# Modulation's products traced a step behind their transfers, and its bias loaded a job ahead

## The chip, the cores and the metric

The kernel runs on one core of a Trainium2 chip. The core has a matrix engine (TensorE, PE in the rows; PEld is its loading of stationary operands), three engines for elementwise work (VectorE or DVE, ScalarE or ACT, GpSimd or POOL) and SyncE (SP), which here only issues DMA transfers. Each engine works through its own queue in order and waits at the head of it for semaphores. The metric is the device time of one execution in microseconds, the median of several runs.

## The reference

The input is a sequence of 256 tokens with 1024 features. Nine sublayers change it in turn: two pre-norm layers (feed-forward, mixer, feed-forward) and one modulated layer (feed-forward, token mixer, feed-forward).

```python
for layer in range(2):
    x = x + 0.5 * swiglu(rmsnorm(x, norm_g[layer, 0]), w_in, w_out)
    x = x + mixer(rmsnorm(x, norm_g[layer, 1]))      # HGRN2, then forgetting attention
    x = x + 0.5 * swiglu(rmsnorm(x, norm_g[layer, 2]), w_in, w_out)

mod = (silu(c) @ w_ada + b_ada).reshape(b, 3, 3, 1024)
def sublayer(h, i, fn, resid_w):
    shift, scale, gate = mod[:, i, 0], mod[:, i, 1], mod[:, i, 2]
    u = rms_norm(h, norm_pre[i]) * (1.0 + scale) + shift
    return h + resid_w * gate * rms_norm(fn(u), norm_post[i])
```

The change touches only `mod`: a vector of 1024 features (c after silu) times a matrix of 1024 x 9216, plus a bias row. All is float32.

## The kernel before

The residual stream stays in SBUF as two tiles of 128 tokens. A projection has the transposed activations as the stationary operand and streams the weights, in k-tiles of 128 rows. For float32's accuracy each operand is split into a high and a low part, and three products go into one accumulator (L208 high by high, L209 with the weights' low part, L210 with the activations' low part). One call of `project` is one token tile by one block of columns: 8 k-tiles, so 24 products. The feed-forward layers take their 2816 hidden columns in slices of 512, 512, 256, 512, 512, 512 (`SLICES`); a slice is four such calls, gate and up for both token tiles.

Weights come in chunks of two k-tiles. `loadw` takes one of five slots of the pool `rawp`, SyncE issues the DMA (L177), ScalarE casts the high part (L166), VectorE subtracts for the low part (L167), in two pieces. The slot is free when the second subtraction is done. Six chunks of high and six of low parts can be held.

The modulation vectors are worked out beside earlier sublayers. `ada` (L840) is a generator for one job of 512 columns: four chunks of `w_ada` (512 KB each, in slots of the same pool), and for each chunk two products on VectorE (L851: `a += raw * cs`, with c spread over the partitions), then a split of `a`, two products with a matrix of ones on TensorE that add up the partitions, and the use of the result (`shift`, `gain` or `post`). The tile `a` is set to zero by GpSimd (L845), and its first row then gets the bias by a DMA (L846). There are 18 jobs: four each in sublayers 3, 5, 6 and 7 (counted from 0) and two in sublayer 8. Sublayer 7 is the token mixer, the others are feed-forward layers. `side` runs one step of the present job, up to its next `yield`: after every `project` of a feed-forward layer from the second slice on, at every fourth item of its output projection, and after the token mixer's projections. A job of before takes five steps: in each of the first four a chunk is loaded and its two products are traced at once, in the fifth `a` is split; the products with ones come with the first step of the next job.

The order of TensorE's instructions is that of the code. The other engines' orders come from a scheduler, which estimates when each instruction could run; SyncE's loads follow the code's order too. `issue_after(x)` is a context in which instructions are queued behind x.

Of the kernel before, what the change touches and what calls it, by code (L numbers as in the profile page):

```python
"""Two pre-norm blocks of two layers (HGRN2 and forgetting attention as mixers), then a
modulated block with stick-breaking and differential attention, on 256 tokens.

Layout: the residual stream stays in SBUF as two tiles of 128 tokens. Every projection has
the activations (transposed, [feature, token]) as the stationary operand and streams the
weights. Both operands are split exactly into a part of float32r's 12 significant bits and
a rest, and hi*hi + hi*lo + lo*hi are summed in PSUM, so each product costs three
single-rate passes at float32's accuracy. The mixers' small products are plain float32.
"""
# [17 lines left out]
D = 1024  # L27
# [6 lines left out]
CK = 2      # k-tiles of 512 columns in a chunk of weights  # L34
# how many tasks of a mixer are under way, the time between their starts and what else their chains take (see weave)
# [3 lines left out]
# (first column, columns) of the hidden slices of a feed-forward layer  # L39
SLICES = ((0, 512), (512, 512), (1024, 256), (1280, 512), (1792, 512), (2304, 512))  # L40

# columns of the array of constants
C_U = 0                 # [128, 9, 128] partial-sum columns: level 128 (first tile), 64..1, 128 (second tile)
C_LM = C_U + 9 * 128    # [128, 7, 64] which scores a level supplies
C_FOXM = C_LM + 7 * 64  # [128, 256] zeros | causal mask
C_SEL = C_FOXM + 256    # [128, 16] -1 in rows h and 32 + h of column h
C_DIST = C_SEL + 16     # [128, 384] -|t - s|, chunk-causal
C_STR = C_DIST + 384    # [128, 384] s < t
C_SUF = C_STR + 384     # [128, 128] -(j > s)
C_WIDE = C_SUF + 128    # [128, 128] the diagonal and the pairs of levels 64 and 32  # L50
# [3 lines left out]
def constants():  # L54
    """Arrays that depend on shapes alone."""
# [12 lines left out]
    c[:, C_FOXM + P:C_FOXM + 2 * P] = np.where(t <= s, 0.0, NEG)   # rows are queries here  # L68
# [3 lines left out]
    for k, (q0, k0) in enumerate(((0, 0), (P, 0), (P, P))):  # L72
        qp, kp = s + q0, t + k0                                    # rows are queries
        c[:, C_DIST + k * P:C_DIST + (k + 1) * P] = np.where(kp // 64 <= qp // 64, -np.abs(qp - kp), -1e34)
    for k, (k0, q0) in enumerate(((0, 0), (0, P), (P, P))):
        c[:, C_STR + k * P:C_STR + (k + 1) * P] = (s + k0) < (t + q0)   # rows are keys
# [5 lines left out]
class Program:  # L82
    """Traces the computation. The order of the tensor engine's instructions is that of this code (the
    other engines are left to the scheduler), so code that feeds it from slower chains is written as
    tasks (generators, see weave) that are woven into the streams of projections."""

    def __init__(self, tc, p, es):
# [34 lines left out]
        self.last_silu = None  # L122
        self.begin = True
        self.jobs = []      # generators that are run beside the projections, a step at a time

    def side(self):
        """A step of the jobs."""
# [37 lines left out]
    def split(self, hi, lo, src):  # L165
        self.nc.scalar.copy(hi, src)  # L166
        self.nc.vector.tensor_sub(lo, src, hi.bitcast(F32))  # L167

    def loadw(self, views, shape, spare=False):
        """One chunk of weights, split: the views side by side in its last dimension. Returns (hi, lo) of its  # L170
# [957 lines left out]
def program(tc, p, stages=None):  # L1128
    """stages: which of the nine sublayers to run (all by default)."""
    stages = list(range(9)) if stages is None else list(stages)  # L1130
    with contextlib.ExitStack() as es:
# [3 lines left out]
        if any(i >= 6 for i in stages):  # L1135
# [5 lines left out]
            for j in sum([plan[s] for s in plan if s not in stages], []):  # L1141
                for _ in j:
                    pass
# [81 lines left out]
```

## Time and profile before

| What | Value |
|---|---|
| Median of 3 runs | 1716.94 us (1714.99 to 1719.26) |
| Profiled execution: span, first to last instruction | 1713.2 us |
| Around the span: median less span | 3.7 us |
| TensorE busy | 1667.1 us, 97% of the span |
| VectorE / ScalarE / GpSimd busy | 67% / 53% / 12% |
| Mean granted TensorE clock | 0.992 of full speed |
| HBM read | 325.86 MB, 191 GB/s over the span |

The page gives the profiled execution's own time as its span; what the median has beyond it (3.7 us) lies outside the first and last instruction. A row of the timeline reads: start, duration, engine, line, operation, tiles written and read, count of merged instructions, and in brackets how long the engine had been idle before it and which instruction ended that. Durations of matmuls are modelled, and overlap; the distance between two starts is what a product costs.

### The profile page before, as it was taken

What the parts mean: (1) busy time and instruction counts of PE and PEld (TensorE: products, weight loads), DVE (VectorE), ACT (ScalarE), POOL (GpSimd) and SP (SyncE); (2) the same over time, 40 slices, a digit from 0 to 9 for tenths busy, and PEclk for the clock granted to TensorE, in tenths of its full rate; (3) what the DMA queues carried; (4) which work ended last, traced back from release to release, by engine and by line L of the source; (5) the groups of instructions that cost most, each with busy time, mean ns of one, the idle gap of its engine ahead of it and who ended that gap; (6) DMA issues with size and microseconds to landing.
All of it is one profiled execution on the core that took longest, in us unless ns stands there. A gap on an engine that the chain in (4) does not pass through costs nothing. (4 is left out here: it accounts for less than half of the span.)

```text
span 1713.2 us, 23351 instructions
## 1 busy us (share of the span) xinstructions
PE 1667.1 (97%) x8136; PEld 1386.2 (81%) x8136; DVE 1144.1 (67%) x2003; ACT 911.8 (53%) x1884; POOL 212.5 (12%) x275
## 2 busy tenths in 40 slices
PE   7999999999999999999999999999999999999998
PEld 5888888788888888888888878878887678778886
DVE  5555587776655677656566767578756678877663
ACT  5545466555544545546665544445545558564452
POOL 2000034330000010003120000110003321120000
PEclk9999999999999999999999999999999999999999
DMA  9555543325656588755345776568764456746652
GB/s 305 177 191 197 183 150 99 99 77 178 212 183 202 172 262 276 238 170 176 122 150 161 242 250 239 167 208 296 256 225 146 159 178 201 248 157 219 226 196 75
DMA packets 176886, 328.45 MB, mean 192 GB/s; under 512 B 12656, under 2 KB 65904, under 8 KB 176768
## 3 DMA queue, kind: packets, MB, share of 16 engines
q1 hardware_dynamic: 173328, 318.29, 56.4%
q0 software_dynamic: 3152, 8.15, 1.7%
q8 instruction: 64, 1.05, 0.2%
q14 instruction: 54, 0.44, 0.1%
q10 hardware_dynamic: 288, 0.52, 0.1%
HBM read 325.86 MB, written 1.05 MB: 191 GB/s over the span
## 5 line engine op out<-in xcount | busy, mean ns | idle before, releaser
L167 DVE TENSOR_TENSOR L<-raw,H 128x512 fp32r<-128x512 f32 (+1 forms) x1092 | 694.9, 681 | 221.6 <-ACT H L166 214.1
L166 ACT CAST H<-raw 128x512 fp32r<-128x512 f32 (+1 forms) x1092 | 599.4, 600 | 426.7 <-PE acc L210 301.8
L208 PE MATMUL acc<-H,uh 128*128 128x512 f32 (+1 forms) x1552 | 600.0, 387 | 1.3 <-ACT uh L166 1.3
L209 PE MATMUL acc<-L,uh 128*128 128x512 f32 (+1 forms) x1552 | 588.5, 379 | 5.9 <-DVE L L167 5.7
L210 PE MATMUL acc<-H,ul 128*128 128x512 f32 (+1 forms) x1552 | 587.0, 378 | 0.5 <-DVE ul L167 0.5
L209 PEld LDWEIGHTS acc<-L,uh 128*128 128x128 f32 x1552 | 294.1, 190 | 61.1 <-DVE L L167 12.0
L210 PEld LDWEIGHTS acc<-H,ul 128*128 128x128 f32 x1552 | 293.5, 189 | 55.5 <-DVE ul L167 1.4
L208 PEld LDWEIGHTS acc<-H,uh 128*128 128x128 f32 x1552 | 294.0, 189 | 52.7 <-ACT uh L166 1.9
L208 PE MATMUL acc<-H,w 128*128 128x512 f32 x536 | 209.8, 391 | 0.0
L209 PE MATMUL acc<-L,w 128*128 128x512 f32 x536 | 208.6, 389 | 0.0
L210 PE MATMUL acc<-H,q 128*128 128x512 f32 x512 | 199.4, 389 | 0.0
L851 DVE SCALAR_TENSOR_TENSOR ad<-raw,cs,ad 128x512 f32<-128x512 f32 x144 | 109.5, 761 | 93.5 <-DMA raw<-in_w_ada 78.6
L209 PEld LDWEIGHTS acc<-L,w 128*128 128x128 f32 x536 | 100.7, 188 | 20.6
L208 PEld LDWEIGHTS acc<-H,w 128*128 128x128 f32 x536 | 100.6, 188 | 20.5
L210 PEld LDWEIGHTS acc<-H,q 128*128 128x128 f32 x512 | 96.1, 188 | 20.1
L276 POOL TENSOR_SCALAR r<-s 128x1 f32<-128x1 f32 x24 | 15.9, 664 | 724.3 <-ACT o L259 482.3
L493 ACT ACTIVATE o<-acc 128x512 f32<-128x512 f32 (+1 forms) x72 | 40.4, 561 | 75.2 <-PE acc L210 75.1
L167 DVE TENSOR_TENSOR q<-T,w 128x512 fp32r<-128x512 f32 (+1 forms) x72 | 43.6, 639 | 45.6 <-ACT w L166 45.6
L233 PE MATMUL T<-ident,o 128*128 128x128 f32 x408 | 55.6, 276 | 14.5 <-DVE o L265 9.7
L498 DVE TENSOR_TENSOR o<-o,acc 128x512 f32<-128x512 f32 (+1 forms) x72 | 45.9, 637 | 34.9 <-PE acc L210 34.7
L233 PEld LDWEIGHTS T<-ident,o 128*128 128x128 f32 x408 | 47.7, 142 | 23.6 <-DVE o L265 9.7
L845 POOL MEMSET ad<- 128x512 f32 x18 | 9.5, 529 | 394.4 <-DVE ad L167 368.7
(244 smaller groups left out, 1440.6 us busy)
## 6 DMA issues: line engine op xcount, KB each, us to landing
raw<-in_ffn_w_in SPq DMA_DIRECT2D x160, 512.0 KB, 4.7
raw<-in_ffn_w_out SPq DMA_DIRECT2D x88, 512.0 KB, 4.2
raw<-in_w_ada SPq DMA_DIRECT2D x72, 512.0 KB, 5.2
raw<-in_ffn_w_down SPq DMA_DIRECT2D x44, 512.0 KB, 4.3
raw<-in_ffn_w_gate SPq DMA_DIRECT2D x40, 512.0 KB, 4.5
raw<-in_ffn_w_up SPq DMA_DIRECT2D x40, 512.0 KB, 4.5
raw<-in_hg_w_in SPq DMA_DIRECT2D x64, 256.0 KB, 3.2
raw<-in_fox_w_in SPq DMA_DIRECT2D x64, 256.0 KB, 3.6
```

The source lines that it names most:

```text
L166: self.nc.scalar.copy(hi, src)
L167: self.nc.vector.tensor_sub(lo, src, hi.bitcast(F32))
L208: mm(out, xh, H, start=first, stop=False)
L209: mm(out, xh, L, start=False, stop=False)
L210: mm(out, xl, H, start=False, stop=last)
L233: self.nc.tensor.transpose(T[:, j, :], src[:, (k0 + j) * P:(k0 + j + 1) * P], self.ident)
L276: self.nc.gpsimd.tensor_scalar(r, s2[:, 0:1], s2[:, 1:2], EPS, op0=ALU.add, op1=ALU.add)
L493: self.last_silu = nc.scalar.activation(s[:, :n], A[:, :n], AF.Silu)
L498: nc.vector.tensor_tensor(s[:, :n], s[:, :n], A[:, :n], op=ALU.mult)
L845: nc.gpsimd.memset(a, 0.0)
L851: nc.vector.scalar_tensor_tensor(a, raw[:, k, :], self.cs[:, k0 + k:k0 + k + 1], a, op0=ALU.mult, op1=ALU.add)
```

## The change

The generator now covers all jobs of a sublayer (`ada(plan[s])`). It loads a chunk at the end of a step, and the chunk's two products are traced at the beginning of the next step. They stand inside `issue_after(last_low)`, where `last_low` is the last low-part subtraction of weights that was traced before. A job takes four steps: its split comes right behind the products of its fourth chunk, and the next job's first chunk and bias are loaded in that same step. The bias goes into row 0 of a constant tile `brow0`, set to zero once at the program's start; the first product of a job reads it in place of `a`, so the 18 fills of `a` are gone. The ones are one column, broadcast. With the comments blanked, lines from L124 on stand one further down in the changed kernel (L167 is L168 there).

```diff
     def split(self, hi, lo, src):
         self.nc.scalar.copy(hi, src)
-        self.nc.vector.tensor_sub(lo, src, hi.bitcast(F32))
+        return self.nc.vector.tensor_sub(lo, src, hi.bitcast(F32))
...
         for (h, l), c in zip(halves, parts):
-            self.split(h, l, raw[c])
+            self.last_low = self.split(h, l, raw[c])
...
-        ones = self.const.tile([P, P], F32R, name="onesr")
+
+        self.brow0 = self.const.tile([P, 512], F32, name="brow0")
+        nc.gpsimd.memset(self.brow0, 0.0)
+        ones = self.const.tile([P, 1], F32R, name="onesr")
         nc.vector.memset(ones.bitcast(F32), 1.0)
-        self.onesr = ones
...
+        self.onesr = ones.to_broadcast([P, P])
+
+    def ada(self, jobs, n=512):
...
-        a = self.tad(n)
-        nc.gpsimd.memset(a, 0.0)
-        nc.gpsimd.dma_start(a[0:1, :], p["b_ada_2"][:, col:col + n])
-        for k0 in range(0, 8, CK):
+
+        def load_b(col):
+            nc.gpsimd.dma_start(self.brow0[0:1, :], p["b_ada_2"][:, col:col + n])
+
+        def load_w(col, k0):
             raw = self.rawp.tile([P, CK, n], F32, name="raw", tag="raw")
             nc.sync.dma_start(raw, p["w_ada_2"][0, k0 * P:(k0 + CK) * P, col:col + n].rearrange("(k p) f -> p k f", p=P))
-            for k in range(CK):
-                nc.vector.scalar_tensor_tensor(a, raw[:, k, :], self.cs[:, k0 + k:k0 + k + 1], a, op0=ALU.mult, op1=ALU.add)
+            return raw
+
+        load_b(jobs[0][0])
+        raw = load_w(jobs[0][0], 0)
+        yield 1
+        for i, (col, use) in enumerate(jobs):
+            a = self.tad(n)
+            for k0 in range(0, 8, CK):
+                with contextlib.ExitStack() as es:
+                    if self.last_low is not None:
+                        es.enter_context(self.tc.issue_after(self.last_low.ins))
+                    for k in range(CK):
+                        nc.vector.scalar_tensor_tensor(a, raw[:, k, :], self.cs[:, k0 + k:k0 + k + 1],
+                                                       self.brow0 if k0 + k == 0 else a, op0=ALU.mult, op1=ALU.add)
+                if k0 + CK < 8:
+                    raw = load_w(col, k0 + CK)
+                    yield 1
+            if i + 1 < len(jobs):
+                load_b(jobs[i + 1][0])
+                raw = load_w(jobs[i + 1][0], 0)
+            s = [self.tad(n, F32R) for _ in range(2)]
+            self.split(s[0], s[1], a)
             yield 1
...
-            b.jobs += plan.get(s, [])
+            b.jobs += [b.ada(plan[s])] if s in plan else []
```

The first place is the 256-column slice of sublayer 3, VectorE's queue: L167 (L168 after) are low parts, with L the weights' and q2 the activations' of the previous slice, and L851 (L869 after) the modulation's products. Before:

```order
L167 TENSOR_TENSOR L_5757<-raw_5754,H_5756 128x256 x2
L498 TENSOR_TENSOR o2_5535<-o2_5535,acc_5603 128x512
L167 TENSOR_TENSOR L_5771<-raw_5768,H_5770 128x256 x2
L851 SCALAR_TENSOR_TENSOR ad_5746<-raw_5811,cs_119,ad_5746 128x512 x2
L851 SCALAR_TENSOR_TENSOR ad_5746<-raw_5841,cs_119,ad_5746 128x512
L167 TENSOR_TENSOR q2_5697<-T_5698,w2_5696 128x512
L851 SCALAR_TENSOR_TENSOR ad_5746<-raw_5841,cs_119,ad_5746 128x512
L167 TENSOR_TENSOR q2_5706<-T_5707,w2_5705 128x512
L167 TENSOR_TENSOR L_5785<-raw_5782,H_5784 128x256 x2
L167 TENSOR_TENSOR L_5799<-raw_5796,H_5798 128x256 x2
```

After, the same slice:

```order
L168 TENSOR_TENSOR L_5773<-raw_5770,H_5772 128x256 x2
L869 SCALAR_TENSOR_TENSOR ad_5750<-raw_5694,cs_119,brow0_122 128x512
L869 SCALAR_TENSOR_TENSOR ad_5750<-raw_5694,cs_119,ad_5750 128x512
L168 TENSOR_TENSOR q2_5701<-T_5702,w2_5700 128x512
L168 TENSOR_TENSOR q2_5710<-T_5711,w2_5709 128x512
L168 TENSOR_TENSOR L_5787<-raw_5784,H_5786 128x256 x2
L168 TENSOR_TENSOR L_5801<-raw_5798,H_5800 128x256 x2
L869 SCALAR_TENSOR_TENSOR ad_5750<-raw_5753,cs_119,ad_5750 128x512 x2
L869 SCALAR_TENSOR_TENSOR ad_5750<-raw_5815,cs_119,ad_5750 128x512 x2
```

Before, the products of the chunks raw_5811 and raw_5841 (four) stand ahead of the last two weight chunks' low parts (L_5785 and L_5799). After, one pair is left there, of the chunk raw_5694, and the next two pairs have moved behind those low parts; the first product of a job reads `brow0`.

In SyncE's queue for the same slice, the loads of `w_ada` (L849, L856 after) and of the weights with 256 columns (L177, L178 after). Before:

```order
L177 DMA raw_5634<-in_ffn_w_in 128x2x256
L177 DMA raw_5648<-in_ffn_w_in 128x2x256
L177 DMA raw_5662<-in_ffn_w_in 128x2x256
L177 DMA raw_5676<-in_ffn_w_in 128x2x256
L849 DMA raw_5749<-in_w_ada_2 128x2x512
L177 DMA raw_5754<-in_ffn_w_in 128x2x256
L177 DMA raw_5768<-in_ffn_w_in 128x2x256
L177 DMA raw_5782<-in_ffn_w_in 128x2x256
L177 DMA raw_5796<-in_ffn_w_in 128x2x256
L849 DMA raw_5811<-in_w_ada_2 128x2x512
L849 DMA raw_5841<-in_w_ada_2 128x2x512
L177 DMA raw_5846<-in_ffn_w_in 128x2x512
```

After:

```order
L178 DMA raw_5633<-in_ffn_w_in 128x2x256
L178 DMA raw_5647<-in_ffn_w_in 128x2x256
L178 DMA raw_5661<-in_ffn_w_in 128x2x256
L178 DMA raw_5675<-in_ffn_w_in 128x2x256
L856 DMA raw_5694<-in_w_ada_2 128x2x512
L856 DMA raw_5753<-in_w_ada_2 128x2x512
L178 DMA raw_5756<-in_ffn_w_in 128x2x256
L178 DMA raw_5770<-in_ffn_w_in 128x2x256
L178 DMA raw_5784<-in_ffn_w_in 128x2x256
L178 DMA raw_5798<-in_ffn_w_in 128x2x256
L856 DMA raw_5815<-in_w_ada_2 128x2x512
L856 DMA raw_5845<-in_w_ada_2 128x2x512
```

Before, one modulation chunk stands ahead of the slice's last four weight chunks and two behind them (raw_5811 and raw_5841, whose products VectorE has ahead of the low parts of raw_5782 and raw_5796, issued earlier). After, two stand ahead and two behind, and the products of raw_5815 come after those of all weights issued before it.

In the token mixer VectorE's L973 (L997 after) feeds GpSimd's L974, which feeds TensorE's L977. Before:

```order
L979 TENSOR_TENSOR w2_12449<-w2_12449,T_12507 128x384
L535 SCALAR_TENSOR_TENSOR w2_12497<-acc_12493,w2_12496 128x384
L851 SCALAR_TENSOR_TENSOR ad_12456<-raw_12801,cs_119,ad_12456 128x512
L973 SCALAR_TENSOR_TENSOR w2_12496<-acc_12493,w2_12496 128x384
L167 TENSOR_TENSOR L_12743<-raw_12739,H_12742 128x512 x2
L851 SCALAR_TENSOR_TENSOR ad_12456<-raw_12801,cs_119,ad_12456 128x512
L979 TENSOR_TENSOR w2_12477<-w2_12477,T_12545 128x384
L535 SCALAR_TENSOR_TENSOR w2_12522<-acc_12518,w2_12521 128x384
L851 SCALAR_TENSOR_TENSOR ad_12456<-raw_12848,cs_119,ad_12456 128x512
```

After, the same heads:

```order
L536 SCALAR_TENSOR_TENSOR w2_12483<-acc_12479,w2_12482 128x384
L997 SCALAR_TENSOR_TENSOR w2_12482<-acc_12479,w2_12482 128x384
L168 TENSOR_TENSOR L_12730<-raw_12726,H_12729 128x512 x2
L1003 TENSOR_TENSOR w2_12463<-w2_12463,T_12532 128x384
L536 SCALAR_TENSOR_TENSOR w2_12508<-acc_12504,w2_12507 128x384
L1003 TENSOR_TENSOR w2_12483<-w2_12483,T_12552 128x384
L997 SCALAR_TENSOR_TENSOR w2_12507<-acc_12504,w2_12507 128x384
L979 COPY q2_12581<-T_12576 64x2x128 x2
L979 COPY q2_12592<-T_12587 64x2x128 x2
L1003 TENSOR_TENSOR w2_12508<-w2_12508,T_12601 128x384
```

The product L851 that stood ahead of the second L973 has gone from this stretch; it comes some ten rows later.

At the program's start ScalarE's queue (L259 and L260 are the second token tile's squares, L166 and L167 casts). Before:

```order
L166 CAST H_168<-raw_166 128x512 x2
L166 CAST uh0_111<-T_138 128x512
L166 CAST uh0_111<-T_145 128x512
L166 CAST H_182<-raw_180 128x512 x2
L259 ACTIVATE o2_152,s2_154<-X1_108 128x512
L259 ACTIVATE o2_153,s2_154<-X1_108 128x512
L166 CAST H_223<-raw_221 128x512 x2
```

After:

```order
L167 CAST H_170<-raw_168 128x512 x2
L167 CAST uh0_111<-T_140 128x512
L167 CAST uh0_111<-T_147 128x512
L167 CAST H_184<-raw_182 128x512 x2
L167 CAST H_225<-raw_223 128x512 x2
L260 ACTIVATE o2_154,s2_156<-X1_108 128x512
L260 ACTIVATE o2_155,s2_156<-X1_108 128x512
L167 CAST H_239<-raw_237 128x512 x2
```

Two casts of a further chunk of weights now stand ahead of the squares of X1. In GpSimd's queue the fill of `brow0` and two instructions for the identity now go ahead of X1's load.

## Rows read from the trace of the kernel before

**Rows 1.** The page's section on busy time, whole execution.
```profile
PE 1667.1 (97%) x8136; PEld 1386.2 (81%) x8136; DVE 1144.1 (67%) x2003; ACT 911.8 (53%) x1884; POOL 212.5 (12%) x275
```

**Rows 2.** The page's costliest groups, modulation's products on VectorE.
```profile
L851 DVE SCALAR_TENSOR_TENSOR ad<-raw,cs,ad 128x512 f32<-128x512 f32 x144 | 109.5, 761 | 93.5 <-DMA raw<-in_w_ada 78.6
```

**Rows 3.** Waits of TensorE: who waited for whom, total us, times, longest us.
```profile
PE T L233 <- DVE o L265: 9.7, 1, 9.7
PE acc L209 <- DVE L L167: 5.7, 12, 1.2
...
PE T L977 <- POOL w L974: 3.9, 3, 1.8
...
PE acc L1008 <- ACT q L962: 1.8, 1, 1.8
```

**Rows 4.** Waits of all engines, those of modulation's products.
```profile
DVE ad L851 <- DMA raw<-in_w_ada: 78.6, 44, 3.5
...
DVE ad L851 <- DMA ad<-in_b_ada: 13.4, 5, 4.8
```

**Rows 5.** Waits of SyncE's queue, the weights' loads.
```profile
SPq L177 <- DVE L L167: 962.4, 437, 14.7
SPq L177 <- DVE ad L851: 87.6, 61, 4.5
```

**Rows 6.** Timeline of VectorE, 256-column slice: start, us, instruction, idle before, releaser.
```profile
626.06 2.33 DVE L851 SCALAR_TENSOR_TENSOR ad<-raw,cs,ad 128x512 f32<-128x512 f32 x3 [1.08 <-DMA raw<-in_w_ada]
...
630.17 1.09 DVE L167 TENSOR_TENSOR L<-raw,H 128x256 fp32r<-128x256 f32 x3
```

**Rows 7.** Timeline of TensorE at the same place.
```profile
629.07 0.28 PE L210 MATMUL acc<-H,ul 128*128 128x256 f32 x1
629.19 0.28 PE L208 MATMUL acc<-H,uh 128*128 128x256 f32 x1
630.64 0.38 PE L209 MATMUL acc<-L,uh 128*128 128x256 f32 x1 [1.17 <-DVE L L167]
630.86 0.28 PE L210 MATMUL acc<-H,ul 128*128 128x256 f32 x1
```

**Rows 8.** One stretch: us, busy of PE, PEld, DVE, ACT, POOL, PEclk, DMA share, GB/s.
```profile
617.00:641.00 24.00, 22.30 (x146) 19.74 (x145) 18.03 (x35) 11.08 (x27) 1.98 (x4) 1.00 0.90 294
```

**Rows 9.** The page's DMA issues: KB each, us to landing.
```profile
raw<-in_ffn_w_in SPq DMA_DIRECT2D x160, 512.0 KB, 4.7
```

**Rows 10.** Timeline of three engines in the token mixer, 1347.5 to 1352 us.
```profile
1348.54 0.75 DVE L851 SCALAR_TENSOR_TENSOR ad<-raw,cs,ad 128x512 f32<-128x512 f32 x1 [1.56 <-DMA raw<-in_w_ada]
...
1349.93 1.28 POOL L974 TENSOR_TENSOR w<-w,mod 128x384 f32<-128x384 f32 x1 [2.29 <-DVE w L973]
...
1351.26 0.91 PE L977 MATMUL T<-w,mod 128*128 128x384 f32 x2 [1.79 <-POOL w L974]
```

**Rows 11.** Timeline of VectorE and TensorE in the token mixer, 1396 to 1402 us.
```profile
1398.46 0.75 DVE L851 SCALAR_TENSOR_TENSOR ad<-raw,cs,ad 128x512 f32<-128x512 f32 x1 [2.56 <-DMA raw<-in_w_ada]
...
1400.85 0.67 PE L1008 MATMUL acc<-q,q 128*128 128x256 f32 x2 [1.76 <-ACT q L962]
```

**Rows 12.** Timeline of GpSimd and TensorE at the token mixer's end, 1474 to 1486 us.
```profile
1475.16 0.53 POOL L845 MEMSET ad<- 128x512 f32 x1 [24.10 <-DVE ad L167]
...
1480.76 0.66 PE L233 MATMUL T<-ident,q 128*128 128x128 f32 x4 [2.22 <-POOL q L1082]
```

**Rows 13.** The page's costliest groups: loads of a usual stationary operand.
```profile
L209 PEld LDWEIGHTS acc<-L,uh 128*128 128x128 f32 x1552 | 294.1, 190 | 61.1 <-DVE L L167 12.0
```

**Rows 14.** Line L784, a broadcast column: count, duration ns min/median/max, first and last start.
```profile
L784 PEld LDWEIGHTS acc<-cT,sel x32: 190/190/192, 800.9 to 890.6; 128*128 128x128 f32 x32
```

**Rows 15.** Timeline of three engines at the start, 0 to 24 us.
```profile
13.01 1.15 ACT L166 CAST H<-raw 128x512 fp32r<-128x512 f32 x2
...
16.54 1.41 DVE L265 SCALAR_TENSOR_TENSOR o<-X,rs,mod 128x512 f32<-128x512 f32 x2
...
17.90 1.03 PE L233 MATMUL T<-ident,o 128*128 128x128 f32 x8
```

More of the change, by code (lines that the diff above doesn't have):

```diff
@@ L122, in __init__ @@
         self.last_silu = None
+        self.last_low = None
         self.begin = True
@@ L836, in ada_start @@
         self.cs = cs
-        ones = self.const.tile([P, P], F32R, name="onesr")
+        self.brow0 = self.const.tile([P, 512], F32, name="brow0")
+        nc.gpsimd.memset(self.brow0, 0.0)
+        ones = self.const.tile([P, 1], F32R, name="onesr")
         nc.vector.memset(ones.bitcast(F32), 1.0)
-        self.onesr = ones
-    def ada(self, col, use, n=512):
+        self.onesr = ones.to_broadcast([P, P])
+    def ada(self, jobs, n=512):
         nc, p = self.nc, self.p
-        a = self.tad(n)
-        nc.gpsimd.memset(a, 0.0)
-        nc.gpsimd.dma_start(a[0:1, :], p["b_ada_2"][:, col:col + n])
-        for k0 in range(0, 8, CK):
+        def load_b(col):
+            nc.gpsimd.dma_start(self.brow0[0:1, :], p["b_ada_2"][:, col:col + n])
+        def load_w(col, k0):
@@ L848, in ada @@
             raw = self.rawp.tile([P, CK, n], F32, name="raw", tag="raw")
             nc.sync.dma_start(raw, p["w_ada_2"][0, k0 * P:(k0 + CK) * P, col:col + n].rearrange("(k p) f -> p k f", p=P))
-            for k in range(CK):
-                nc.vector.scalar_tensor_tensor(a, raw[:, k, :], self.cs[:, k0 + k:k0 + k + 1], a, op0=ALU.mult, op1=ALU.add)
-            yield 1
-        s = [self.tad(n, F32R) for _ in range(2)]
-        self.split(s[0], s[1], a)
-        yield 1
-        T = self.bank()
@@ L857, in ada @@
-        for j in range(2):
-            nc.tensor.matmul(T[:, :n], self.onesr, s[j], start=j == 0, stop=j == 1)
-        use(T[:, :n])
+            return raw
[19 more added lines that the diff above has]
+            self.split(s[0], s[1], a)
+            yield 1
+            T = self.bank()
+            for j, x in enumerate(s):
+                nc.tensor.matmul(T[:, :n], self.onesr, x, start=j == 0, stop=j == 1)
+            use(T[:, :n])
@@ L881, in use @@
                                                    op0=ALU.add if part == 1 else ALU.mult, op1=ALU.mult)
-            return self.ada((3 * i + part) * D + h * 512, use)
+            return (3 * i + part) * D + h * 512, use
         return tiles, [[job(part, h) for h in range(2)] for part in range(3)]
@@ L1140, in program @@
             b.ada_start()
-            for j in sum([plan[s] for s in plan if s not in stages], []):
-                for _ in j:
-                    pass
+            for s in plan:
+                if s not in stages:
+                    for _ in b.ada(plan[s]):
+                        pass
         def norm_of(s):
```

## The prediction

> **What bounds the kernel now.** The page's busy times come first: TensorE is busy for 1667.1 of 1713.2 us, no other engine for more than 67% [rows 1]. So only the 46.1 us in which TensorE stands still are there to be won, and the waits of TensorE, read next, say whom it waits for [rows 3]. Most of that has nothing to do with modulation: 9.7 us is the program's first wait. Two kinds can. Twelve waits of 5.7 us in all are for a low part of weights, the work that shares VectorE's queue with modulation's 144 products; by windows of the trace all twelve lie in the four feed-forward sublayers with jobs. Two single waits in the token mixer, 1.8 us each, follow a product of modulation. The waits of all engines show why: VectorE stands 78.6 us at the head of its queue for a chunk of `w_ada` (44 times) and 13.4 us for a bias (5 times), and whatever is queued behind stands too [rows 4]. Most of those 92.0 us cost nothing, since six chunks of low parts are held ahead of TensorE.
>
> The timelines of VectorE and of TensorE at one of the twelve places show the whole step. VectorE idles 1.08 us for the chunk, then runs three products in 2.33 us, and the weights' low parts come at 630.17 [rows 6]. TensorE had its last product at 629.19 and goes on at 630.64 [rows 7].
>
> **The change part by part.**
>
> *Products behind the last split, a step late.* At this place the order shows that the products of the last-loaded chunk have moved behind the low parts of all weights issued before it. The price of a wait: products of 256 columns start 0.12 us apart (629.07 to 629.19); here the distance is 1.45, so 1.33 are lost where the row says 1.17 idle; the next distance is 0.22, another 0.10 [rows 7]. So a wait costs its idle time and some 0.26, and the twelve together 5.7 + 12 x 0.26 = 8.8 us [rows 3, 7]. At most all of it goes (-8.8), at least nothing, because a low part may be late for another reason: its own chunk landed late, or its slot came free late. SyncE waits 962.4 us in 437 waits for slots that a low part of weights frees, and 87.6 us in 61 for slots that a modulation product frees [rows 5]. The change makes the second kind longer: a chunk now keeps its slot for a whole step, and SyncE's weights are queued behind that. In the stretch of the 256-column slice the transfers already take 0.90 of the DMA engines [rows 8]. I take two thirds, -5.9, nearer to the whole, because at the place that I can read the lateness (1.17) is less than the time that modulation held the queue (1.08 + 2.33), and because in slices of 512 columns a step lasts twice as long and the slots suffice. The third left over is for the slices of 256.
>
> The Trainium skill, "DMA: Bandwidth & Descriptors", section Rules for kernel authors, asks for just this: issue a transfer early, do other work, and wait late. By it the whole of the twelve waits would go, and the sum would be lower by 2.9. That rule says nothing of the slot that an early transfer holds; the rows of SyncE's waits do, and no run shown here holds a chunk that long.
>
> *The same in the token mixer.* At 1348.54 a product that had waited 1.56 us stands ahead of the step of VectorE that feeds GpSimd, and TensorE waits 1.79 for that [rows 10]. At 1398.46 one that had waited 2.56 us stands ahead of the copies of queries, and TensorE waits 1.76 [rows 11]. In the order after, the first has gone ten rows down, and the second now stands behind both pads. I take both, 1.79 + 1.76 = -3.5; with the restart of 0.26 each it is -4.1, and 0 if other chains are late there instead.
>
> *The bias a job ahead, no fills.* The five waits for a bias (13.4 us on VectorE) go, since the row now has four steps to land; what they cost TensorE is within the twelve waits above. GpSimd loses 17 of 18 fills of 0.53 us each [rows 12]. The one at 1475.16 stands ahead of the gates' products at the token mixer's end, where TensorE later waits 2.22 for one of them [rows 12]; that wait follows VectorE's own product, so I take 0 and keep -2.2 as the far end. A new wait comes in return: the row's next load must wait until the first product of a job has read `brow0`. That load stands in GpSimd's queue; behind it are the norms' small steps. It is issued three steps after that product, so I take 0; one GpSimd wait of the size seen, +1.8 [rows 3], is the far end.
>
> *Ones as a broadcast column.* The same 36 products; a stationary operand from a broadcast column loads in 190 ns [rows 14], a usual one in 190 [rows 13]. Nothing.
>
> *Four steps per job.* The same loads, denser by a quarter, and the same 144 products of 0.76 us [rows 2]; VectorE is 67% busy [rows 1], so this is paid in lateness alone, which is in the two thirds above.
>
> *The start.* The fill of `brow0` (0.53, by the other fills) delays the load of X1 on GpSimd, and ScalarE's two casts of one chunk, 1.15 us, now go ahead of X1's squares. Before, the norm starts at 16.54, with its first half (0.70 of 1.41) done at 17.24, and TensorE comes to the transposes at 17.90 [rows 15]: 0.66 of slack. So 1.15 - 0.66 = +0.5; at most +1.2, if the slack is lost to other casts, and 0 if the estimate of the scheduler is right and the chunk arrives first anyhow.
>
> Sum against the profiled execution: -5.9 - 3.5 + 0.5 = -8.9, so a span of 1704.3; with the 3.7 us between the span and the median of the runs shown, **1708.0 us**.
>
> **The rivals.**
>
> *The stalls only move.* In the slice of 256 columns twelve loads are to arrive in four calls of 24 x 0.12 = 2.9 us; the transfers are the limit there (0.90 busy [rows 8]), and an order on VectorE can't make them faster. Then the 8.8 stay, the token mixer gives 3.5 and the start costs up to 1.2: 1716.9 - 2.3 = 1714.6. For it: the DMA share of that stretch, and the 78.6 us of VectorE's waits themselves, which say that chunks are late. Against: the products at 626.06 were three in a row ahead of weights issued before them, which is order, not transfer.
>
> The Trainium skill, the same page, section Issuing engines are not separate DMA queues, says that all transfers run on the same 16 engines and interleave, so an earlier chunk of `w_ada` takes its time from a weight's. The share of 0.90 agrees with it in that stretch; by it this rival's 1714.6 or the next one's time would come.
>
> *Slower: slots.* Two chunks of modulation now stand ahead of each four of weights and are held for a step, so weights may run on three of five slots. A weight chunk takes 4.7 us to land [rows 9] and some 1.1 for its split (three pieces take 1.09 [rows 6]): 5.8 / 3 = 1.93 us per chunk, where TensorE in the 256-column slice uses one per 11.5 / 8 = 1.44. That is 0.49 late per chunk, 3.9 in a slice, 15.7 in the four sublayers, and with 32 restarts of 0.26 24.0. It replaces the 8.8; with -3.5 and +0.5 the sum is +12.2: 1729. It decides from the point where two chunks are held while weights are waited for; with four slots the pace is 5.8 / 4 = 1.45, just enough. In slices of 512 TensorE uses a chunk per 2.9, and three slots do. For it: SyncE already waits for slots nearly everywhere [rows 5]. Against: the chunks are loaded before the slice's weights, land early, and VectorE frees them within a call.
>
> *Larger.* All twelve waits go (-8.8), both in the mixer with their restarts (-4.1), the gates' wait too (-2.2), and the start costs nothing: -15.1, 1701.8.
>
> *The change doesn't do what it says:* the products could still be early. The order speaks against it at all places that I read, so it gets no more than 0.02, with the time of before.
>
> **How the numbers follow.** Forecast 0.55 (1704 to 1712), the stalls only move 0.24, larger 0.09, slower 0.10, no effect 0.02. What a measurement here can tell from no change is 0.3%, 5.2 us: faster is below 1711.8, slower above 1722.1. Faster: the larger case and most of the forecast's, 0.09 + 0.53 = 0.62; slower 0.10; the rest, 0.28, is the same. The range reaches down to the larger case, with the runs' own spread of about 2 us below it (1714.99 beside 1716.94), 1700; and up over the rival in which stalls move, with the same spread, 1717. About 0.15 lie above it, 0.03 below.
>
> **What would show it.** Right: the waits of L209 for weights' low parts fall from twelve to four or so, in the 256-column slices; no wait near 1348 and 1398 follows a product of modulation; VectorE's waits for chunks fall to a few us and those for a bias to none; SyncE's waits for slots of modulation grow above 87.6. The start: the first product of the second token tile about 0.5 later. Wrong: as many waits of L209 as before, now ended by a cast that waited for its transfer (stalls move), or SyncE's long waits on modulation's slots followed by TensorE's waits in every such slice (slots).

## The result, and the profile after

The changed kernel takes 1730.17 us (median of 4 runs, 1728.46 to 1733.09) beside 1716.93 for the kernel before on the same chip: ratio 1.008 (1.0062 to 1.0099). It is slower by 13 us where 9 us less were forecast. The profiled execution has a span of 1727.5 us.

The waits of TensorE, in the kernel after (columns as in [rows 3]; L209, L210 and L211 are L208, L209 and L210 of before, L882 the products with ones, L998 and L1001 are L974 and L977 of before):

```profile
PE acc L209 <- ACT H L167: 7.5, 3, 3.4
...
PE T L1001 <- POOL w L998: 4.3, 2, 3.0
...
PE T L882 <- ACT ad L167: 2.7, 1, 2.7
...
PE acc L210 <- DVE L L168: 1.5, 6, 0.3
...
PE T L882 <- DVE ad L168: 1.2, 1, 1.2
```

The waits for a low part have fallen from 5.7 us in twelve to 1.5 in six [rows 3]. In their place TensorE waits 7.5 us in three for a high part, which is a chunk that came late, and 3.9 us for the split of a modulation vector, which it never did before. VectorE no longer stands for modulation; the page's group, after (first the products that read `a`):

```profile
L869 DVE SCALAR_TENSOR_TENSOR ad<-raw,cs,ad 128x512 f32<-128x512 f32 x126 | 95.6, 759 | 1.8 <-DMA raw<-in_w_ada 0.3
```

The 78.6 us of [rows 4] are 0.3 now. They had cost little, and what took their place costs more. SyncE's waits after:

```profile
SPq L178 <- DVE L L168: 1027.5, 456, 14.7
SPq L178 <- DVE ad L869: 64.0, 46, 5.2
SPq L856 <- DVE L L168: 57.5, 46, 11.4
```

The waits for slots that a modulation product frees have fallen in all (87.6 before [rows 5]), though the longest has grown from 4.5 to 5.2, and those on weights' low parts are 65 us longer.

TensorE's products stand in the same order in both kernels, apart from the 36 with ones. So the start of each product can be compared with the start of the same product before, and the difference read at the borders of the sublayers. Each figure is how much longer (or shorter) that part of the kernel takes than in the profiled execution of before, worked out from the two traces, one execution each. In e3 and e9 the orders of the engines are the same through sublayer 3, and the figures there are 3.6 and 0.6: a single figure can be off by 3 us, so the medians of the runs count first. The columns 3, 5, 6, 8 are the feed-forward sublayers with modulation beside them, 7 is the token mixer:

```
kernel                      start  0-2     3     4     5     6     7     8   all
after                        0.2  -0.1   4.1  -0.1  -2.7   4.9   5.9   2.1  14.3
bias only (e1)              -0.1  -2.4   4.7  -0.1  -0.3   2.7   0.1   1.7   6.3
products only (e2)          -0.1  -2.4   3.2  -0.1  -1.9   5.8   6.1   1.0  11.6
five steps (e3)              0.5  -1.3   3.6  -0.1  -5.9   3.3   3.4  -1.4   2.0
no queueing (e4)            -0.1  -0.1   5.6  -0.1   0.3   4.1  -1.7   0.5   8.6
big loads late (e5)          0.4  -1.3   2.9  -0.1  -1.7   2.2   5.2   1.4   9.0
mixer not queued (e6)        0.0  -0.8   3.7  -0.1  -2.8   5.7  -0.8   1.3   6.2
before, loads later (e7)    -0.4   0.2   1.7  -0.1   0.2   3.3  -0.7  -0.4   3.9
five, late, free (e8)        0.5  -0.7  -2.6  -0.1  -5.9   0.8  -2.9  -1.7 -12.6
five, free (e9)              0.5   0.0   0.6  -0.1  -5.8   2.3   3.1  -1.4  -0.8
no steps in 256 (e10)        0.5  -0.8  -1.7  -0.1  -5.8  -1.7   5.3  -1.5  -5.8
five, late, free, 256 (e11)  0.7  -1.2  -3.0   0.4  -5.8  -1.8  -3.5  -1.4 -15.6
before, four slots (e12)     0.4  -0.4   4.9  -0.1   4.8   5.1   3.0   2.5  20.2
```

So the change gained in sublayer 5, and lost in 3, 6, 8 and most in the token mixer. How it lost in sublayer 3 is seen in the following views. Two stretches of the same work (the 256-column slice), first before, then after; columns as in [rows 8]:

```profile
611.00:624.00 13.00, 13.00 (x73) 11.32 (x72) 8.63 (x19) 4.65 (x14) 6.34 (x12) 1.00 0.85 271
624.00:637.00 13.00, 11.83 (x90) 11.16 (x89) 9.64 (x18) 8.13 (x19) 0.00 (x0) 1.00 0.87 281
```

```profile
613.00:625.00 12.00, 12.00 (x72) 10.64 (x72) 7.76 (x17) 4.54 (x13) 0.02 (x1) 1.00 0.64 198
625.00:637.00 12.00, 8.76 (x73) 8.46 (x71) 6.28 (x13) 3.43 (x9) 5.71 (x11) 0.94 0.86 296
637.00:645.00 8.00, 8.00 (x23) 6.12 (x24) 6.83 (x13) 3.88 (x7) 0.00 (x0) 0.66 0.89 304
```

Before, the transfers are busy 0.85 and 0.87. After, 0.64 and then 0.86: twelve microseconds in which too little is loaded, and then not enough time. In the first half SyncE waits for slots. Its timeline and VectorE's, after:

```profile
612.92 1.04 SPq L856 DMA_DIRECT2D raw<-in_w_ada  x2
618.12 5.03 SPq L178 DMA_DIRECT2D raw<-in_ffn_w_in  x4
...
623.95 0.74 DVE L869 SCALAR_TENSOR_TENSOR ad<-raw,cs,brow 128x512 f32<-128x512 f32 x1
624.72 0.75 DVE L869 SCALAR_TENSOR_TENSOR ad<-raw,cs,ad 128x512 f32<-128x512 f32 x1
...
627.93 1.53 DVE L869 SCALAR_TENSOR_TENSOR ad<-raw,cs,ad 128x512 f32<-128x512 f32 x2
```

Two chunks of modulation are issued by 613.96 (raw_5694 and raw_5753 in the order shown with the change), then nothing until 618.12. VectorE is done with the first at 625.47 and with the second at 629.46, 12 and 16 us after their issue, where a call of this slice takes 2.9. So the next slice's weights start later. SyncE's timeline, before and after:

```profile
625.01 6.30 SPq L177 DMA_DIRECT2D raw<-in_ffn_w_in  x4
```

```profile
627.37 4.37 SPq L178 DMA_DIRECT2D raw<-in_ffn_w_in  x4
```

Why so much is asked for in the second half is seen in GpSimd's timeline, first before, then after:

```profile
613.16 0.60 POOL L846 DMA_DIRECT2D ad<-in_b_ada  x1 [0.29 <-POOL ad L845]
613.77 0.57 POOL L247 DMA_DIRECT2D mod<-in_norm_pre  x1
614.33 0.53 POOL L247 DMA_DIRECT2D mod<-in_norm_g  x1
```

```profile
624.98 0.49 POOL L852 DMA_DIRECT2D brow<-in_b_ada  x1 [25.88 <-DVE ad L869]
625.51 0.57 POOL L248 DMA_DIRECT2D mod<-in_norm_pre  x1
626.07 0.54 POOL L248 DMA_DIRECT2D mod<-in_norm_g  x1
```

The bias of the third job has stood in GpSimd's queue for 25.88 us, for the product that reads the second one's row. Behind it stand the rows and constants of the following sublayers, two of them 512 KB, which before went out 12 us earlier. The next slice's weights share the transfers with them; the DMA issues after, 612 to 640 us:

```profile
raw<-in_w_ada SPq DMA_DIRECT2D x6, 512.0 KB, 5.2
raw<-in_ffn_w_in SPq DMA_DIRECT2D x4, 512.0 KB, 9.2
...
mod<-in_norm_pre POOLq DMA_DIRECT2D x1, 512.0 KB, 7.2
```

Those four chunks take 9.2 us to land, beside 4.7 over the whole kernel before [rows 9]. ScalarE and TensorE after, the same place:

```profile
636.33 1.14 ACT L167 CAST H<-raw 128x512 fp32r<-128x512 f32 x2 [7.69 <-DMA raw<-in_ffn_w_in]
...
637.00 0.80 PE L209 MATMUL acc<-H,uh 128*128 128x512 f32 x1 [3.25 <-ACT H L167]
```

TensorE stands 3.25 us, and then the granted clock is 0.66 on average over the next 8 us (the stretch 637 to 645 above). Against the same products of before, 6.2 us are lost by 642.54, where products come at the full pace again.

In the token mixer the products with ones come before the split that they need; TensorE and ScalarE after:

```profile
1487.83 0.50 PE L882 MATMUL T<-ad,onesr 128*128 128x512 f32 x1 [2.65 <-ACT ad L167]
1489.53 0.80 PE L882 MATMUL T<-ad,onesr 128*128 128x512 f32 x1 [1.19 <-DVE ad L168]
```

```profile
1486.14 1.12 ACT L167 CAST H<-raw 128x512 fp32r<-128x512 f32 x2
1487.17 0.61 ACT L167 CAST ad<-ad 128x512 fp32r<-128x512 f32 x1
```

The split stands behind two casts of weights. From the last product ahead of these waits to the first behind them 5.1 us are lost, and 1.1 more in slower products. But the wait for the gates of [rows 12], which comes next before, is gone, with slower products behind it: 5.4 us come back, and this place is +0.8 in all. Three other places cost more. TensorE waits 2.98 us for GpSimd, where a product of modulation stands ahead of L997 in VectorE's queue:

```profile
1382.41 1.42 DVE L869 SCALAR_TENSOR_TENSOR ad<-raw,cs,ad 128x512 f32<-128x512 f32 x1
...
1386.41 1.51 PE L1001 MATMUL T<-w,mod 128*128 128x384 f32 x2 [2.98 <-POOL w L998]
```

It waits 1.7 for copies of queries (L1051). And 2.7 of the 5.9 come at the stage's start, where one multiplication of GpSimd (L262) took 4.68 us; in every other run it took 1.6 to 1.7, so this is not put down to the change.

### The profile page after: what moved, and what is told of

Its sections match the earlier page's. It is cut to its first block, busy times and chain, and to the rows that moved or that the text cites. A ratio compares the mean times of both kernels' runs of the same rounds, so it can differ in the third digit from the quotient of the medians.

```text
span 1727.5 us, 23272 instructions
## 1 busy us (share of the span) xinstructions
PE 1673.9 (97%) x8136; PEld 1392.2 (81%) x8136; DVE 1142.4 (66%) x2003; ACT 915.6 (53%) x1884; POOL 204.4 (12%) x258
## 5 line engine op out<-in xcount | busy, mean ns | idle before, releaser
L168 DVE TENSOR_TENSOR L<-raw,H 128x512 fp32r<-128x512 f32 (+1 forms) x1092 | 696.9, 679 | 285.2 <-ACT H L167 276.7
L167 ACT CAST H<-raw 128x512 fp32r<-128x512 f32 (+1 forms) x1092 | 601.2, 600 | 453.9 <-PE acc L211 305.6
L209 PE MATMUL acc<-H,uh 128*128 128x512 f32 (+1 forms) x1552 | 602.8, 388 | 8.7 <-ACT H L167 7.5
L210 PE MATMUL acc<-L,uh 128*128 128x512 f32 (+1 forms) x1552 | 589.5, 380 | 1.5 <-DVE L L168 1.5
L211 PE MATMUL acc<-H,ul 128*128 128x512 f32 (+1 forms) x1552 | 589.1, 380 | 1.0 <-DVE ul L168 1.0
L209 PEld LDWEIGHTS acc<-H,uh 128*128 128x128 f32 x1552 | 295.6, 190 | 61.5 <-ACT H L167 8.6
L211 PEld LDWEIGHTS acc<-H,ul 128*128 128x128 f32 x1552 | 294.5, 190 | 56.7 <-DVE ul L168 1.9
L210 PEld LDWEIGHTS acc<-L,uh 128*128 128x128 f32 x1552 | 295.5, 190 | 54.3 <-DVE L L168 4.3
L209 PE MATMUL acc<-H,w 128*128 128x512 f32 x536 | 209.7, 391 | 0.0
L210 PE MATMUL acc<-L,w 128*128 128x512 f32 x536 | 208.6, 389 | 0.0
L211 PE MATMUL acc<-H,q 128*128 128x512 f32 x512 | 199.3, 389 | 0.0
L209 PEld LDWEIGHTS acc<-H,w 128*128 128x128 f32 x536 | 100.6, 188 | 20.6
L210 PEld LDWEIGHTS acc<-L,w 128*128 128x128 f32 x536 | 100.7, 188 | 20.4
L211 PEld LDWEIGHTS acc<-H,q 128*128 128x128 f32 x512 | 96.1, 188 | 20.1
L869 DVE SCALAR_TENSOR_TENSOR ad<-raw,cs,ad 128x512 f32<-128x512 f32 x126 | 95.6, 759 | 1.8 <-DMA raw<-in_w_ada 0.3
L168 DVE TENSOR_TENSOR q<-T,w 128x512 fp32r<-128x512 f32 (+1 forms) x72 | 43.2, 640 | 60.6 <-ACT w L167 60.6
L618 POOL TENSOR_TENSOR w<-w,w 128x512 f32<-128x512 f32 (+1 forms) x32 | 45.9, 1452 | 41.3 <-ACT w L616 41.2
```

Of the source, the lines that this page charges most:

```text
L168: return self.nc.vector.tensor_sub(lo, src, hi.bitcast(F32))
L209: mm(out, xh, H, start=first, stop=False)
L210: mm(out, xh, L, start=False, stop=False)
L211: mm(out, xl, H, start=False, stop=last)
L618: nc.gpsimd.tensor_tensor(eq[:, i0:, :], e[:, i0:, :], qT[:, None, :].to_broadcast([P, 4 - i0, P]), op=ALU.mult)
L869: nc.vector.scalar_tensor_tensor(a, raw[:, k, :], self.cs[:, k0 + k:k0 + k + 1], self.brow0 if k0 + k == 0 else a, op0=ALU.mult, op1=ALU.add)
```

## The experiments

The theories were: A, the big loads that are held up behind the bias in GpSimd's queue; B, slots that modulation's chunks hold for a step; C, four steps a job in place of five; D, the queueing of products behind the last split.

**e1, the bias alone.** The steps of before; the first product reads `brow0`, the next bias is loaded behind a job's last products.

```diff
         for i, (col, use) in enumerate(jobs):
             a = self.tad(n)
             for k0 in range(0, 8, CK):
-                with contextlib.ExitStack() as es:
-                    if self.last_low is not None:
-                        es.enter_context(self.tc.issue_after(self.last_low.ins))
...
-                if k0 + CK < 8:
-                    raw = load_w(col, k0 + CK)
-                    yield 1
+                raw = load_w(col, k0)
...
+                yield 1
             if i + 1 < len(jobs):
                 load_b(jobs[i + 1][0])
-                raw = load_w(jobs[i + 1][0], 0)
```

> The steps of the kernel before (five a job, products traced with their chunk's load, not queued behind weights), with the bias alone a job ahead in the row of zeros. Theory A (queue of GpSimd: the next bias waits for the first product that read the row, and the constants of the next sublayer queue behind it, so that 1.5 MB of transfers land in the 256-column slice): those constants start after 620 us instead of 613.8 in sublayer 3, and the time is 1720 to 1727. Theory B (slots: a chunk that is held for a step takes slots from weights): no chunk is held here, the five waits for a bias are gone, 1714 to 1718. Theory C (four steps a job): as B.

Measured: 1722.87 us, ratio 1.003 (1.0015 to 1.0045). The bias alone costs, most in sublayers 3 and 6; in 3 the big loads start at 616.3 us in place of 613.8 (not after 620, as A had it). They are 1.2 MB there, not the 1.5 that the expectation says. Chunks of modulation land late then (VectorE waits 107.1 us for them, before 78.6), and since their products still stand ahead of weights, TensorE waits for VectorE; its waits in e1:

```profile
PE acc L210 <- DVE L L168: 13.8, 9, 5.5
```

**e2, the products alone.** The tile `a` filled with zeros and its bias loaded, as before, but right behind the split of the job before.

```diff
-            nc.gpsimd.dma_start(self.brow0[0:1, :], p["b_ada_2"][:, col:col + n])
+            a = self.tad(n)
+            nc.gpsimd.memset(a, 0.0)
+            nc.gpsimd.dma_start(a[0:1, :], p["b_ada_2"][:, col:col + n])
...
```

> The changed kernel's steps and queueing, with the bias as before: the tile of a job filled with zeros and its row loaded, traced right behind the split of the job before. Theory A: the constants of sublayer 4 start before 620 us again, TensorE's waits of several us for a high part of weights (7.5 us in three) fall to under 3, and the time is 1718 to 1723. Theory B: these waits stay, 1727 to 1733. Theory C: 1727 to 1733 too.

Measured: 1728.04, ratio 1.0066 (1.0046 to 1.0086). Without the row of zeros most of the loss is there, so it doesn't come from that row. A is not refuted by this, since its condition did not come about: the big loads start at 622.4 and not before 620, behind the fill, which waits for the present job's split.

**e3, five steps.** A step between the last products and the split.

```diff
+            yield 1
             if i + 1 < len(jobs):
                 load_b(jobs[i + 1][0])
```

> The changed kernel with five steps a job: the products of the fourth chunk, then a step, then the split and the next job's loads. Theory A: the constants still queue behind the bias, 1726 to 1731, with only the 3.9 us waits of the products with ones in the token mixer gone. Theory B: one chunk in five steps less is held beside weights, about a fifth of the losses in the feed-forward layers goes, 1725 to 1730. Theory C (density): 1715 to 1720.

Measured: 1714.25, ratio 0.9984 (0.9968 to 1.0): 16 us less than the changed kernel, by one line. C had this, just above. Sublayers 5 to 8 gain against the changed kernel, and the waits for the split of a modulation vector are gone. Sublayers 3 and 6 stay at +3.6 and +3.3.

**e4, no queueing.**

```diff
-                with contextlib.ExitStack() as es:
-                    if self.last_low is not None:
-                        es.enter_context(self.tc.issue_after(self.last_low.ins))
...
```

> The changed kernel without the context that queues the products behind the last split of weights; they are still a step behind their load. Theory A: the constants queue as in the changed kernel, 1727 to 1732. Theory B: products run as soon as VectorE has room, slots come free earlier, 1720 to 1726. Theory D (the queueing itself delays the products and with them slots and the products with ones): as B, and TensorE's wait of 2.7 us for a split of modulation in the token mixer goes.

Measured: 1723.78, ratio 1.0037 (1.0016 to 1.0058). The token mixer goes from +5.9 to -1.7: there the queueing is the cause (D). In the feed-forward sublayers without it 3 and 5 are worse (+5.6, +0.3), and 6 and 8 slightly better.

**e5, the big loads late.** The large tiles get a tiny fill on VectorE, queued behind a later split of weights; their loads wait for it.

```diff
+    def hold(self, b, j=1):
+        if self.mark is not None:
+            with self.tc.issue_after(self.mark[j].ins):
+                self.nc.vector.memset(b[:, 0:1], 0.0)
...
```

> The changed kernel, in which the big loads of rows and constants for the next sublayers (norm rows of 512 KB, the mixers' constants) wait for a tiny fill on VectorE that is queued behind the weights' splits of the 256-column slice (the gain's row) or of the slice after it (the others). Theory A (these loads, held back by the bias's wait in GpSimd's queue, fall into the 256-column slice and take its weights' transfers): TensorE's three waits for a high part of weights (7.5 us) fall to one of 1 to 3 us, sublayers 3 and 6 lose 1 us each against before in place of 4.1 and 4.9, and the time is 1721 to 1725. Theory B (slots held by modulation's chunks): those sublayers stay at +3 to +5, 1728 to 1732.

The marks stood one slice later than the expectation says (behind the slice after the 256-column one, and the next). Measured: 1721.84, ratio 1.0034 (1.0017 to 1.0052). The loads start at 651 and 675 us; sublayers 3 and 6 lose 2.9 and 2.2 in place of 4.1 and 4.9. But the loss has moved with the loads. At the end of the 256-column slice of sublayer 3 TensorE no longer stops; it stops behind the load at 651, for a chunk that was issued right after it and took 8.0 us to land:

```profile
651.07 0.56 POOL L254 DMA_DIRECT2D mod<-in_norm_pre  x1 [8.32 <-DVE mod L249]
...
660.30 0.50 PE L210 MATMUL acc<-H,uh 128*128 128x512 f32 x1 [1.14 <-ACT H L168]
```

In sublayer 6 it is the same, behind the load at 1191.6. So the 2.9 and 2.2 are no measure of B.

**e6, no queueing in the token mixer.**

```diff
-                    if self.last_low is not None:
+                    if self.last_low is not None and self.queued:
...
```

> The changed kernel with the queueing behind the last split left out in the token mixer alone. Theory D (there the queueing puts products, and with them the split and the products with ones, behind work that TensorE is ahead of): the token mixer's loss of 5.9 us becomes none or a gain of 1 to 2, 1722 to 1725. Theory C (four steps a job: the products with ones come one step after the last chunk's products in any case): the waits of 2.7 and 1.2 us stay and the time is 1727 to 1731.

Measured: 1720.82, ratio 1.0031 (1.001 to 1.0052). The token mixer is at -0.8 where it was at +5.9: D, as expected (the median is 9 us lower).

**e7, the kernel before with the big loads later.** The same fill, behind the last split of the 256-column slice itself (the expectation says one slice earlier); modulation as before.

```diff
             before = (c0, n)
+            if c0 == 1024:
+                self.mark = [self.last_low] * 2
...
```

> The kernel before, modulation untouched, in which only those big loads wait for a tiny fill behind the last split of the slice ahead of the 256-column one, so that they start some 6 to 12 us later than before. Theory A: sublayers 3 and 6 lose 3 to 5 us each, 1722 to 1727. Theory B: no loss, 1714 to 1719.

Measured: 1716.27, ratio 1.0006 (0.9981 to 1.003). The loads start at 632 us. Sublayers 3 and 6 lose 1.7 and 3.3 in the profiled execution, but the median shows no loss: A is not shown to cost anything by itself. The loads come seven microseconds later here than in the changed kernel, when the first chunk of the next slice has landed.

**e8, five steps, big loads late, no queueing in the token mixer.** The edits of e3, e5 and e6 together.

> Five steps a job, the big loads late as in the run of that name, no queueing in the token mixer. If A, C and D each hold and add up: from the 1714.25 of five steps, 5 to 6 off in sublayers 3 and 6 and 3 to 4 in the token mixer, 1704 to 1708. If A is wrong 1710 to 1713; if D is wrong too 1713 to 1717.

Measured: 1702.32, ratio 0.9933 (0.9906 to 0.9959), below what was expected. Sublayer 3 is at -2.6 where five steps alone had +3.6.

**e9, five steps, no queueing in the token mixer.** The edits of e3 and e6.

> Five steps a job and no queueing in the token mixer, the big loads left where the bias puts them. If A holds on top of five steps: sublayers 3 and 6 keep +3.6 and +3.3 against before, the token mixer goes from +3.4 to -2.9, and the time is 1707 to 1709. If the gain of the run with late loads came from the mixer alone: 1701 to 1704.

Measured: 1710.6, ratio 0.9958 (0.9938 to 0.9977), 8 us above e8 and above both ends of what was expected. The profiled executions show 3.2 and 1.5 of the difference in sublayers 3 and 6, no more than what two executions of the same orders differ by; e9 has three waits for a high part there (3.2 us), e8 one (1.7). 6.0 are in the token mixer (+3.1 against -2.9), which the expectation did not have; one wait of 1.8 us for the copies of queries came back there. What of its order makes that was not tried.

**e10, no step of modulation in the 256-column slice.** The changed kernel, with four steps a job and all else as it was.

```diff
-            if c0:
+            if c0 and c0 != 1024:
                 self.side()
```

> The changed kernel with no step of modulation in the four calls of the 256-column slice; its jobs go on four steps later. If the losses of sublayers 3, 6 and 8 are there because modulation's chunks and the loads behind its bias share that slice's transfers and slots (A and B together): these three go to between -2 and +1 against before, the token mixer's +5.9 stays, 1720 to 1724. If four steps a job cost as such, wherever they fall: the losses move to the slice after it and the time stays at 1727 to 1731.

Measured: 1710.75, ratio 0.9958 (0.9938 to 0.9977): 19 us less than the changed kernel and 9 below what was expected. Sublayers 3, 6 and 8 go from +4.1, +4.9, +2.1 to -1.7, -1.7, -1.5, as expected if that slice is the place, and sublayer 5 gains 3 more. The token mixer stays at +5.3. No wait for a high part of weights is left. The big loads move too, to 642 us, so A and B are not told apart here. The two stretches of before, in e10:

```profile
611.00:624.00 13.00, 13.00 (x74) 11.36 (x73) 6.60 (x16) 4.29 (x13) 0.00 (x0) 1.00 0.57 171
624.00:637.00 13.00, 13.00 (x94) 12.27 (x93) 9.88 (x18) 7.46 (x16) 0.00 (x0) 1.00 0.77 248
```

TensorE is busy throughout, with transfers at 0.57 and 0.77.

**e11, e8 without steps in that slice.**

> The run with five steps, late loads and no queueing in the token mixer, and no step of modulation in the 256-column slice either. If the last wait for a high part (1.7 us, sublayer 6) and the small ones there are due to that slice: 1699 to 1702. If the steps that move to the output projection make new waits: 1703 to 1708.

Measured: 1697.79, ratio 0.9872 (0.9834 to 0.9909), the fastest here: 19 us below the kernel before, and below both ends of what was expected.

**e12, the kernel before with four slots.**

```diff
-        self.rawp = pool("raw", 5)
+        self.rawp = pool("raw", 4)
```

> The kernel before with four slots for weights and modulation chunks in place of five. If a slot that is away costs as much as theory B says (the changed kernel holds one or two for a step): in the four feed-forward sublayers with modulation 3 to 6 us each are lost, most of it in and right behind the 256-column slice, and little (under 1 us) in the two feed-forward sublayers without; 1727 to 1740. If slots are not what weights wait for, and only the transfers' collision counts: 1715 to 1720.

Measured: 1734.78, ratio 1.0094 (1.0058 to 1.013). The loss is 4.9, 4.8, 5.1 and 2.5 us in the four feed-forward sublayers with modulation, 3.0 in the token mixer, and nothing in sublayers 0 to 2 and 4. A slot is worth that where modulation's chunks share the pool, and nothing where weights have it alone. So B has a price in the kernel before; that the changed kernel pays it is not shown by this run, since sublayer 5, which loses 4.8 here, gained 2.7 there.

**What the traces add.** The traces show how slots and big loads act together. For the first chunk of weights of the slice behind the 256-column one, the table gives how much later it is issued than in the kernel before (against the same products of TensorE), its time to landing, and how long TensorE then stops ahead of that slice, all in us and worked out from the traces:

```
               sublayer 3             sublayer 6
           later  landing  stop   later  landing  stop
before        0      4.6     0       0      5.9     0
after       2.3      8.9   3.4     4.6      9.1   3.6
e1         -2.2     10.0     0     0.1      7.8     0
e2          4.5      6.3   3.1     6.8      6.0   2.7
e3          2.2      4.0     0     4.6      4.0     0
e5          2.4      5.0     0     4.6      5.3     0
e6          2.4      9.8   4.5     4.6      8.9   3.4
e8          2.2      3.6     0     4.6      4.1     0
```

A chunk that is late by its slot alone (e3, e5, e8) doesn't stop TensorE here; one that is late and also lands slowly does (after, e2, e6). That a slow landing alone wouldn't is not shown: in e1 TensorE had stopped for a low part just before (5.5 us in sublayer 3), which gave the chunk that time. In sublayers 5 and 8 the changed kernel issues that chunk 5.0 and 5.3 us later, with no load of rows or constants beside it: it lands in 5.5 and 6.1, and TensorE stops 0 and 0.9 us. So the held slots use up the lead of the weights, and the big loads make the stop of it.

## Why the prediction was wrong

*The low parts.* Right in kind: the twelve waits went to six, 5.7 us to 1.5. The sum stopped there. It read two thirds of a gain from the waits that go, and for "the third left over" took at worst the waits of before. What is late next was a high part: a chunk not in time at all. This is the step that failed first: the term was given a floor of nothing gained, and no new wait. The four feed-forward sublayers with modulation have +8.4 where the term had -5.9. The price of such a wait was also unlike that of [rows 7]: 3.25 idle cost 6.2, with products 0.43 us apart behind it, where idle time and 0.26 make 3.5.

*Slots.* The text had the mechanism, its place and its point of decision in the rival on the other side, at 0.10 and 1729 us. The place was right (the 256-column slice and the chunks behind it), e10 and the table above bear the slots out as one half of the cause, and the time is near, but by luck: its sum isn't the one that came: for the four feed-forward sublayers it had 24.0 - 8.8 = +15.2, measured are 4.1 - 2.7 + 4.9 + 2.1 = +8.4. Its reason against, that chunks "land early, and VectorE frees them within a call", did not hold in the shortest calls (12 and 16 us from issue to the last use, in sublayer 3). The arithmetic of that rival (three slots 1.93 us per chunk, TensorE 1.44) was better evidence than the one place from which the share of two thirds was taken; [rows 5] and [rows 8] spoke for it.

*The token mixer.* Forecast -3.5, measured +5.9. Both waits read there did shrink: the one of [rows 10] by 1.9 us against the product before, that of [rows 11] by 0.9. But moved products came to stand ahead of other steps of the same kinds (3.0 us for GpSimd, 1.7 for copies of queries), which the term had as its own far end, "0 if other chains are late there instead". And the products that are queued behind the last split come late for their own consumer: 3.9 us of waits for a split of a modulation vector. Nothing in the prediction asked who waits for the products themselves. Without the queueing there the mixer is at -0.8 (e6). With four steps a job the products with ones come one step after the last chunk, and that step was taken as free.

*The bias.* "Behind it are the norms' small steps" is wrong: behind it are 1.2 MB of rows and constants in sublayer 3, as GpSimd's timeline says. And "issued three steps after that product" holds for the code's order only: GpSimd came to that load 25.88 us before the product had run. Taken at 0, with 1.8 as the far end, it costs 5.7 us alone (1722.87 beside 1717.17, e1).

*Four steps a job.* "Paid in lateness alone, which is in the two thirds above": it is 16 us, the difference between the changed kernel and e3, which shares in the losses named above and is not to be added to them.

*The start.* +0.5 forecast, +0.2 measured, by luck: the first product comes 1.2 us earlier, which nothing in the prediction had, and 1.4 go again at the second token tile's transposes, where TensorE now waits 1.59 us, and after. That is above the far end of 1.2.

*The broadcast column* was taken as nothing; no run tries it alone.

What stays open: how much of the feed-forward loss outside these stops goes to either, since the smaller waits were not followed one by one; and what in the token mixer's order costs e9 6.0 us more than e8.

## What to carry to other kernels

A transfer that is issued earlier and used later holds its buffer longer: before counting the waits that go, count the buffers per consumer's pace in the shortest stage, here twelve loads in five slots. Two delays that are each covered can stop the consumer when they fall on the same chunk. Work that is moved off a critical queue has a consumer too, so ask when that comes. And a load that gets a new wait takes along everything behind it in its queue, which the order shows by name; the size of the next transfers behind it matters more than its own.

## What was not expected of the hardware

After TensorE stood idle for 3.25 us its products of 512 columns started 0.43 us apart, the lower of its two levels (1.2 GHz; at 2.4 they start 0.23 apart); the kernel after:

```profile
638.74 0.63 PE L209 MATMUL acc<-H,uh 128*128 128x512 f32 x1
639.17 0.63 PE L210 MATMUL acc<-L,uh 128*128 128x512 f32 x1
```

The granted clock was 0.66 on average over those 8 us. After the 1.17 us of [rows 7] it stayed at 1.00 [rows 8]. Between executions the HGRN2 sublayer, which no edit touches, differed by up to 2.4 us (the column 0-2), and sublayer 3 by 3.0 between e3 and e9, so a part of one trace says less than the medians.
